# Swapping the quadrants of a matrix by DMA: transfers of consecutive rows, and transfers of every eighth row

## The chip, the cores and the metric

The kernel runs on one core of one Trainium2 chip. It uses none of the core's compute engines for the work itself: the data goes from device memory (HBM) to device memory through the core's 16 DMA engines. The metric is the device time of one execution in microseconds; a kernel's figure is the median of several executions.

## The reference

The input is one float32 matrix of 8192 rows and 8192 columns, 268.44 MB (a row is 32 KB). The reference is

```python
def reference(x: np.ndarray) -> np.ndarray:
    return np.fft.ifftshift(x)
```

With even sizes this shifts both axes by half: the upper left quadrant of 4096 x 4096 changes places with the lower right one, and the upper right with the lower left. Nothing is computed. Half a row, 4096 floats or 16 KB, is the longest run that stays together both in the input and in the output, and every one of the 16,384 half rows moves to another place.

## The kernel before

The program is one loop with no tiles in on-chip memory and no arithmetic. It names four things: `hr` and `hc`, half the number of rows and of columns (4096 each), `col`, the column half of the upper output rows that is being written, and `other`, the opposite column half.

The outer loop (line 28) goes over the upper 4096 output rows in blocks of `ROWS_PER_DMA` = 512 rows, eight blocks. The inner loop (line 29) goes over the two column halves. Each pass issues two transfers. The one on the sync engine's queue (line 31) writes the block in the upper half of the output, from the input rows 4096 further down and the other column half. The one on the scalar engine's queue (line 35) writes the mirror image: the same block of rows in the lower half of the output, from the upper half of the input. So there are 8 x 2 = 16 transfers on each queue, each of 512 half rows of 16 KB, 8 MB in all. Inside a transfer the half rows lie 32 KB apart, on the reading and on the writing side, since the other half of each row belongs to the next transfer of the queue. The second pass of the inner loop takes the same rows with the column halves exchanged.

The order of the work is set by the two queues alone. The two engines issue their transfers in program order, and both queues are served by the same 16 DMA engines. No transfer needs data from another. Each queue has four completion semaphores in turn; a transfer that takes one up again waits until the transfer four places before it on the queue has landed. A transfer ends with one completion write from each of the 16 DMA engines. At the end of the program (the end of the block that begins at line 64) the sync engine waits for the last transfers. Lines 53 and 64 belong to the launch code, which also fills four small constants at the start.

Of the kernel before, what the change touches and what calls it, by code (L numbers as in the profile page):

```python
# [1 line left out]

# [4 lines left out]


ROWS_PER_DMA = 512  # L10


@with_exitstack
def kernel(
    ctx: ExitStack,
    tc: tile.TileContext,
    x: bass.AP,
    out: bass.AP,
):


    nc = tc.nc

    R, C = x.shape
    hr = R // 2
    hc = C // 2

    for row in range(0, hr, ROWS_PER_DMA):
        for col in (0, hc):
            other = hc - col  # L30
            nc.sync.dma_start(
                out=out[row : row + ROWS_PER_DMA, col : col + hc],
                in_=x[row + hr : row + hr + ROWS_PER_DMA, other : other + hc],
            )
            nc.scalar.dma_start(
                out=out[row + hr : row + hr + ROWS_PER_DMA, other : other + hc],
                in_=x[row : row + ROWS_PER_DMA, col : col + hc],
            )


# [1 line left out]
_INS = ['x']  # L42
_OUTS = [((8192, 8192), 'float32')]


def kernel(**inputs):
    import numpy as _np
    import concourse.bacc as _bacc
    import concourse.tile as _tile
    from concourse import mybir as _mybir  # L50
    from concourse.bass_utils import run_bass_kernel_spmd as _run

    nc = _bacc.Bacc("TRN2", target_bir_lowering=False, num_devices=1)  # L53
    arrays, args = {}, []
    for name in _INS:
        a = _np.ascontiguousarray(inputs[name])
        if a.dtype.kind in "iu":
            a = a.astype(_np.int64)
        arrays[f"in_{name}_dram"] = a
        args.append(nc.dram_tensor(f"in_{name}_dram", a.shape, _mybir.dt.from_np(a.dtype), kind="ExternalInput").ap())  # L60
    for i, (shape, dtype) in enumerate(_OUTS):
        dt = _mybir.dt.from_np(_np.dtype(dtype))
        args.append(nc.dram_tensor(f"out_{i}_dram", shape, dt, kind="ExternalOutput").ap())
    with _tile.TileContext(nc) as tc:
        kernel(tc, *args)
    r = _run(nc, [arrays], core_ids=[0])
    got = tuple(r.results[0][f"out_{i}_dram"] for i in range(len(_OUTS)))
    return got[0]
```

## Time and profile before

| what | value |
|---|---|
| median of 4 runs | 812.24 us (811.9 to 812.93) |
| the profiled execution's own time | 812.93 us |
| its span, first to last instruction | 811.1 us |
| DMA packets | 16,896, with 268.44 MB read and as much written |
| mean rate, each byte counted once | 331 GB/s |
| rate of reads and writes together | 662 GB/s |
| transfers | 16 on each of two queues, 8192 KB each |
| median time from issue to landing | 201.5 us (sync), 201.6 us (scalar) |

The profile is of one execution. The span is cut into 40 equal slices of about 20 us; the row marked DMA gives the mean busy share of the 16 engines in tenths (9 means 90% or more), the row marked GB/s what they moved, with each byte counted once. A packet here is one half row of 16 KB, or a completion write of a few bytes. The share of a queue is the time that its packets took as a part of 16 engines' span. The trace also holds, for each packet, its start, duration, size and queue, and for each transfer the times of its 16 completion writes. It holds no addresses. The issue list gives the median time from the issue of a transfer to its landing.

### The profile page before, as it was taken

To read this page: it belongs to the slowest core of one execution; us is meant where nothing else is said; L and a number is where in the kernel's file an instruction comes from. 1 tells how busy PE (TensorE), PEld (TensorE's weight loads), DVE (VectorE), ACT (ScalarE), POOL (GpSimd) and SP (SyncE) were. 2 spreads that over 40 slices of the span, in tenths; PEclk is the share of its full clock that TensorE was granted. 3 is DMA by queue.
4 is the path that set the end of the run, shared out by engine and by line. 5 is a ranking of instruction groups with operands and counts; after the bars stand their busy time and mean duration, and the time that the engine had idled before them with its cause. 6 is when DMAs were issued, how large, how long until landed. Compare 5 with 4: busy or idle time off the path is not lost. (4 is left out here: it accounts for less than half of the span.)

```text
span 811.1 us, 77 instructions
## 1 busy us (share of the span) xinstructions
POOL 0.2 (0%) x4
## 2 busy tenths in 40 slices
POOL 0000000000000000000000000000000000000000
DMA  9999999999999999999999999999999999999998
GB/s 309 333 330 334 335 329 327 339 330 334 335 328 334 334 334 330 334 338 333 334 333 330 336 335 337 332 334 331 331 337 330 332 334 328 330 334 334 337 335 271
DMA packets 16896, 268.44 MB, mean 331 GB/s; under 512 B 512, under 2 KB 512, under 8 KB 512
## 3 DMA queue, kind: packets, MB, share of 16 engines
q1 hardware_dynamic: 8448, 134.22, 50.4%
q10 hardware_dynamic: 8448, 134.22, 48.8%
HBM read 268.44 MB, written 268.44 MB: 662 GB/s over the span
## 5 line engine op out<-in xcount | busy, mean ns | idle before, releaser
L53 POOL MEMSET const-bfloat16-1.0<- 128x1 bf16 x1 | 0.1, 103 | 0.0
L53 POOL MEMSET const-uint8-127<- 128x1 uint8 x1 | 0.1, 103 | 0.0
L53 POOL MEMSET const-float32-1.0<- 128x1 f32 x1 | 0.1, 100 | 0.0
L53 POOL MEMSET const-float32-0.0<- 128x1 f32 x1 | 0.1, 99 | 0.2 <-issue 0.2
## 6 DMA issues: line engine op xcount, KB each, us to landing
out_dram<-in_x_dram ACTq DMA_DIRECT2D x16, 8192.0 KB, 201.6
out_dram<-in_x_dram SPq DMA_DIRECT2D x16, 8192.0 KB, 201.5
```

The lines of the kernel that those rows point to most:

```text
L53: nc = _bacc.Bacc("TRN2", target_bir_lowering=False, num_devices=1)
```

## The change

The number of transfers, their size and the queue of each output half stay as they are. What changes is which rows make up one transfer. Before, a transfer takes 512 consecutive rows of one column half, 32 KB apart. After, it takes every eighth row of the upper (or lower) 4096 rows: 512 rows that lie `STEP * C` = 65,536 floats, 256 KB, apart, so that one transfer reaches over the whole height of its half. The outer loop runs over the eight starting rows `c`, the inner one over the two column halves, and for each the sync queue gets the upper output half and the scalar queue the lower one. The access patterns are written by hand from an offset and the dimensions `dims`: 512 rows with the 256 KB step, and 4096 consecutive floats of each.

```diff
-ROWS_PER_DMA = 512
+STEP = 8
...
-    for row in range(0, hr, ROWS_PER_DMA):
+    dims = [[STEP * C, hr // STEP], [1, hc]]
+    for c in range(STEP):
         for col in (0, hc):
-            other = hc - col
-            nc.sync.dma_start(
-                out=out[row : row + ROWS_PER_DMA, col : col + hc],
-                in_=x[row + hr : row + hr + ROWS_PER_DMA, other : other + hc],
-            )
-            nc.scalar.dma_start(
-                out=out[row + hr : row + hr + ROWS_PER_DMA, other : other + hc],
-                in_=x[row : row + ROWS_PER_DMA, col : col + hc],
-            )
+            for eng, r0, h in ((nc.sync, 0, col), (nc.scalar, hr, hc - col)):
+                eng.dma_start(
+                    out=bass.AP(out.tensor, out.offset + (r0 + c) * C + h, dims),
+                    in_=bass.AP(x.tensor, x.offset + (hr - r0 + c) * C + hc - h, dims),
+                )
```

## The prediction

> **What bounds the kernel now.** I read the page's head and its second and third parts first, to see whether anything but transfers takes time, then the DMA issues, the waits of the sync engine's queue, and the transfer rate in chosen windows.
>
> ```profile
> span 811.1 us, 77 instructions
> ...
> POOL 0.2 (0%) x4
> ...
> DMA  9999999999999999999999999999999999999998
> GB/s 309 333 330 334 335 329 327 339 330 334 335 328 334 334 334 330 334 338 333 334 333 330 336 335 337 332 334 331 331 337 330 332 334 328 330 334 334 337 335 271
> DMA packets 16896, 268.44 MB, mean 331 GB/s; under 512 B 512, under 2 KB 512, under 8 KB 512
> ...
> q1 hardware_dynamic: 8448, 134.22, 50.4%
> q10 hardware_dynamic: 8448, 134.22, 48.8%
> HBM read 268.44 MB, written 268.44 MB: 662 GB/s over the span
> ...
> out_dram<-in_x_dram ACTq DMA_DIRECT2D x16, 8192.0 KB, 201.6
> out_dram<-in_x_dram SPq DMA_DIRECT2D x16, 8192.0 KB, 201.5
> ```
>
> No engine computes; the 16 DMA engines have a packet in flight for 50.4 + 48.8 = 99.2% of the span. The packets are 16,384 rows of 16 KB and 512 small ones (32 transfers, each ending in 16 completion writes). 99.2% of 16 x 811.1 us over 16,384 packets is 786 ns a packet. So the time is the number of packets times the packet's duration, over 16; nothing else is on the path except the ends.
>
> ```profile
> SPq L64 <- DMA out_dram<-in_x_dram: 164.8, 2, 117.5
> SPq L31 <- DMA out_dram<-in_x_dram: 128.9, 12, 49.6
> ```
>
> The sync queue waits, but for transfers four places back: its first four issue without waiting, the other 12 once an earlier one has landed. With 201.5 us from issue to landing and one landing about every 50 us on each queue, the engines never run dry. These waits cost nothing.
>
> Next the windows: stretch, length, the only busy engine, clock, DMA share, GB/s (each byte counted once).
>
> ```profile
> 2.00:4.00 2.00, 0.00 (x0) 1.00 0.99 360
> 4.00:6.00 2.00, 0.00 (x0) 1.00 1.07 385
> 6.00:10.00 4.00, 0.00 (x0) 1.00 0.95 340
> 10.00:20.00 10.00, 0.00 (x0) 1.00 1.00 329
> 20.00:800.00 780.00, 0.00 (x0) 1.00 1.00 333
> 552.00:556.00 4.00, 0.00 (x0) 1.00 0.93 291
> 556.00:560.00 4.00, 0.00 (x0) 1.00 1.11 393
> ```
>
> The middle 780 us run at 333 GB/s; the rest of the span is 31.1 us of ends. The packet records behind these rows say what sets the rate. The shortest 16 KB packet takes 608 ns and 39% take under 650; the median is 727, the 75th percentile 906, the 90th 1,066, the mean 785. A DMA engine that met nobody would take about 611 ns, so about 174 ns of each packet is waiting in memory on other packets. This is the only term that the change can touch.
>
> **The change part by part.** *Count, size, issue.* 8 offsets x 2 column halves x 2 queues are again 32 transfers of 512 rows of 16 KB: the same bytes and packets, 16 issues a queue, the same two queues and alternation of column halves. Cost zero, covered by the four transfers queued ahead. Were the cover gone, an issue plus the start of its packets would show: the first issue begins at 0.73 us, the first packet at 2.20, so 1.5 us a transfer.
>
> *The wait between transfers.* The tail is alike: the last landings, at 808.5 us (sync) and 810.3 (scalar), would again be those of 8 MB transfers whose 16 completions come within 1.1 to 3.5 us of each other. Cost zero.
>
> *The rows in flight together.* This is the change. Those 1.1 to 3.5 us are one or two steps of an engine, which takes a row from each queue every 2 x 786 ns: the 16 engines walk their 32 rows nearly in step. The profile has no addresses, so how rows are dealt is open. If in blocks, engines now stand 32 rows = 1 MiB apart and step by 32 KB; afterwards 8 MiB apart, stepping by 256 KB. If in turn, 32 KB becomes 256 KB between engines. Either way, in one stage of about 100 us (two column halves of one offset) every row read or written on both queues afterwards has the same place, one in eight, within its 256 KB. Now the places in use at one moment differ by the engines' spread and by the sync queue's lead over the scalar queue (about 4 to 5 us in landings, near three steps), and over a transfer all eight come up. If place in 256 KB helps choose which part of memory serves a row, the change makes more rows meet there; the higher address bits must then keep them apart.
>
> No row of this profile has a 256 KB step, so I bound the price. From below: every packet at the unhindered 611 ns gives 16,384 x 0.611 / 16 = 626 us, too far to be a case; every packet at the median, 727, gives 744. From above: at the 75th percentile, 928 us; at the 90th, 1,092. To each belongs the 6.8 us of span without packets (811.1 - 804.3, the packet times summed over 16). The nearer rows are stretches of this same mix. Of the 195 windows of 4 us between 20 and 800 us (291 and 393 above are near the extremes; counting packets by when they end) the slower half averages 323 GB/s, the faster half 343, the fastest quarter 349. I take the slower half as a lasting state: 780 x 333 / 323 = 804.1 us in the middle, plus 31.1 of ends = 835.2 us span, +24.1. It means 24 ns more waiting per packet, 174 to 198: a seventh more contention. I choose the loss over the gain because the edit removes variety among the addresses in flight and adds none that I can name; and the small end of loss because the engines drift freely and can move out of each other's way.
>
> Outside the span the profiled execution has 812.93 - 811.1 = 1.8 us, and it stands 0.7 above the median of the four runs, 812.24. So 835.2 + 1.8 - 0.7 = 836 us.
>
> Two pages of the Trainium skill bear on the size. "DMA: Bandwidth & Descriptors", section "Latency and other measured facts", reports that copies of 16 KiB rows lose rate at large power-of-two pitches (207 GB/s at 512 KiB, 164 at 2 MiB, 103 at 4 and 8 MiB, 214 with a padded pitch), and calls the cause, streams in step on the same memory channels, an inference. Taking its mildest loss, 207/214, an estimate by that page would be 839 us; taking the 8 MiB figure for the distance between engines would double the time. "HBM Reference", section "Specifications (TRN2)", gives about 716 GB/s per memory domain; the 662 read above is 92% of it, and by that figure no order of rows could bring the transfers below some 750 us.
>
> **The rivals.**
> *Faster: the wider step keeps engines apart.* Place: the 174 ns of waiting in the middle stretch. For it: the first full window, when all engines have just started in step, runs at 385 GB/s and the rate falls to 329 by 10 to 20 us, so arrangement matters and the present mix is not the best. Against it: a 2 us window scatters by 25 GB/s, so 385 is two such scatters. Price at the faster half's rate: 780 x 333 / 343 + 31.1 = 788.4, less 22.7, so 790 us; at the fastest quarter's, 776. It decides as soon as the mean packet falls under 784 ns.
> *No change: the addresses are mixed well anyway.* For it: the 20 us slices, all between 324 and 338, show no dependence on where in the matrix the transfers are. 812 us.
> *Deep conflict.* The rows of a stage fall on few parts of memory and the engines cannot drift out of it. For it: 8 MiB between engines leaves only high address bits to tell them apart. Against it: the engines have four transfers queued, so one that falls behind need not hold the others. Price: from the 75th to the 90th percentile packet, 936 to 1,100 us with what lies around.
> *The transfers of a queue wait for each other*, because their row ranges now interlace and the framework sees a conflict. Each of 15 later transfers on a queue would then add the 1.5 us start and up to 3 us of ragged end: 68 us, 880 us in all, or nothing where the other queue fills the gap. Against it: the two column halves of a transfer pair interlace already, and the first four issues a queue do not wait.
>
> **How the numbers follow.** About 0.2%, 1.6 us, is what a measurement here can tell from no change. Moderately slower, 814 to 940: 0.45. Deep conflict, above 940: 0.12. Queue waits: 0.03. No change: 0.10. Faster: 0.30, of which 0.06 lies below 777, the fastest quarter's rate. Slower is then 0.60, same 0.10, faster 0.30. The range 777 to 940 leaves out 0.18. Of the slower cases alone the likeliest's own range is 814 to 940, the upper end the 75th percentile packet.
>
> **What would show it.** Right: 16,896 packets and x16 issues of 8192 KB a queue as now, the DMA row still all 9s, the shortest packet still near 608 ns, but the slices around 323 GB/s instead of 333 and fewer packets under 650 ns. Wrong in sign: slices above 335 with more packets at the floor. Zeros or dips in the DMA row at each landing, or waits on the transfer just before, would mean queue waits. A rate that changes with the offset stage, about every 100 us, would show that the place in 256 KB matters by itself. The forecast fails most easily at the sign: it rests on an argument about addresses that no row here shows.

## The result and the profile after

The changed kernel takes 811.38 us (median of 53 executions, 810.79 to 812.47), the kernel before 813.61 us in the same comparison (79 executions, 809.0 to 819.31). The ratio is 0.9972, 95% interval 0.9964 to 0.998: faster by 0.28% (2.2 us between the medians), just beyond what such a measurement can tell from no change. The forecast was 836 us, slower. Ratios given with an interval compare the faster executions of each kernel, so they can differ from the ratio of the medians.

The difference is one of steadiness: of the 79 executions of the kernel before, 56 are slower than the slowest of the changed kernel (812.47 us), but 7 are faster than its fastest (810.79 us).

These are the rows of the page of the changed kernel that answer to those shown of before: head, busy share of the DMA engines, rate, packets, queues and issues.

```profile
span 809.8 us, 77 instructions
...
DMA  9999999999999999999999999999999999999999
GB/s 308 330 333 334 332 333 333 328 334 335 335 333 333 331 337 329 336 331 337 319 337 333 337 334 333 333 333 335 329 334 334 333 330 337 335 333 331 337 329 302
DMA packets 16896, 268.44 MB, mean 332 GB/s; under 512 B 512, under 2 KB 512, under 8 KB 512
...
q1 hardware_dynamic: 8448, 134.22, 49.8%
q10 hardware_dynamic: 8448, 134.22, 49.8%
HBM read 268.44 MB, written 268.44 MB: 663 GB/s over the span
...
out_dram<-in_x_dram ACTq DMA_DIRECT2D x16, 8192.0 KB, 201.5
out_dram<-in_x_dram SPq DMA_DIRECT2D x16, 8192.0 KB, 201.4
```

Packets, issues and the time to landing are as they were. The difference is in the last slice (302 GB/s against 271 before) and in the queue shares: the packets' time, 99.6% of 809.8 = 806.6 us, is 2.0 us more than before (99.2% of 811.1 = 804.6), and the part of the span without packets (averaged over the 16 engines) falls from 6.5 to 3.2 us. The net is the 1.3 us between the spans.

The windows of the changed kernel (stretch, length, busy engine, clock, DMA share, GB/s) say the same.

```profile
2.00:4.00 2.00, 0.00 (x0) 1.00 0.99 287
4.00:6.00 2.00, 0.00 (x0) 1.00 1.06 434
6.00:10.00 4.00, 0.00 (x0) 1.00 1.02 356
10.00:20.00 10.00, 0.00 (x0) 1.00 1.00 326
20.00:800.00 780.00, 0.00 (x0) 1.00 1.00 333
800.00:812.00 12.00, 0.00 (x0) 1.00 0.64 217
```

The last row has this counterpart before:

```profile
800.00:812.00 12.00, 0.00 (x0) 1.00 0.61 206
```

The middle moves at 333 GB/s in both. Between the 1,000th and the 16,000th half row to end, the packet records give 333.14 GB/s before and 333.06 after. The completion times of the last transfer on each queue show what became of the end (us from the span's start; first, median and last of the 16 engines):

```
              sync queue              scalar queue
before   805.0   805.7   808.5    807.3   808.1   810.3
after    806.0   806.5   806.8    807.9   808.6   808.9
```

The typical engine of the changed kernel finishes a little later, its last engine 1.4 us earlier. This holds all the way through: the 16 completions of a transfer lie 1.1 to 3.5 us apart before and 0.5 to 1.4 us after. The sync queue's waits did not change in kind.

```profile
SPq L62 <- DMA out_dram<-in_x_dram: 165.1, 2, 117.2
SPq L33 <- DMA out_dram<-in_x_dram: 131.6, 12, 50.0
```

So for this pair of executions the gain is at the end. It is not the whole story, as three more traces of the kernel before show below.

### The profile page after: what moved, and what is told of

Same layout as the page of the kernel before. It is cut to its first block, busy times and chain, and to the rows that moved or that the text cites. A ratio compares the mean times of both kernels' runs of the same rounds, so it can differ in the third digit from the quotient of the medians.

```text
span 809.8 us, 77 instructions
## 1 busy us (share of the span) xinstructions
POOL 0.2 (0%) x4
```

## The experiments

Each comparison is with the kernel before on the same chip; its median beside the first group (the next four runs) was 822.17 us, beside the others 813.5 to 814.7. The record gives the same chip number, 8, for the first group and for one of the later ones, so why the first is 1% slower (329 GB/s in the middle of its two traces of the same row order, in place of 333) is open; that shift is larger than the gain of the change, and the changed kernel itself was not run there. The diffs are shortened: a loop and its body stand on one line, and `move(start, dims)` stands for the changed kernel's two inner loops, with the starting row and the access pattern as arguments. In a pattern such as `[[256 * C, 16], [C, 32], [1, hc]]` the first pair makes 16 groups of rows, 256 rows apart, the second the 32 rows of a group; the rows of a group are taken to go to one engine (in the run with eight groups eight engines took part). The step between the rows that an engine takes one after another is called its walk.

```diff
+    def move(start, dims):
         for col in (0, hc):
             for eng, r0, h in ((nc.sync, 0, col), (nc.scalar, hr, hc - col)):
                 eng.dma_start(
-                    out=bass.AP(out.tensor, out.offset + (r0 + c) * C + h, dims),
-                    in_=bass.AP(x.tensor, x.offset + (hr - r0 + c) * C + hc - h, dims),
+                    out=bass.AP(out.tensor, out.offset + (r0 + start) * C + h, dims),
+                    in_=bass.AP(x.tensor, x.offset + (hr - r0 + start) * C + hc - h, dims),
                 )
```

**Groups 8 MiB apart, walking 32 KB.**

```diff
-    for c in range(8): move(c, [[8 * C, 512], [1, hc]])
+    for b in range(8): move(32 * b, [[256 * C, 16], [C, 32], [1, hc]])
```

> Each transfer takes 16 groups of 32 consecutive half rows, the groups 8 MiB apart: the spacing between engines of the changed kernel if rows are dealt in blocks, with the 32 KB step of the kernel before. Theory A (shared ceiling: memory gives all reads and writes together about 666 GB/s, whichever rows are in flight): the middle stays at 333 GB/s and the time within 0.4% of before, 809 to 815 us; only the ends can differ. Theory B (which rows meet sets the rate, and the 256 KB step happens to be as good as 32 KB): a new mix gives a new rate, more than 1% away. If the wide spacing between engines is what lets them finish together, the 16 completion writes of a transfer come within about 1 us of each other, as in the changed kernel (0.5 to 1.4 us), and the time is about 0.2 to 0.3% below before; if the 256 KB step is the cause, they spread to about 3 us as before and the time is that of before.

Measured: 1,802.33 us (median of six executions, 1,753 to 1,882), 2.19 times before by the medians; the ratio of the faster executions is 2.136 (2.1266 to 2.1454). The completions of a transfer lie 3.1 to 5.1 us apart. The page of an execution of 1,808 us:

```profile
span 1806.6 us, 77 instructions
...
DMA  8989999999999999999989899999999999999999
GB/s 143 159 147 150 147 147 153 141 151 146 145 153 142 152 150 147 155 146 158 142 149 153 139 157 145 152 150 147 151 144 150 152 144 155 150 145 151 148 153 135
DMA packets 16896, 268.44 MB, mean 149 GB/s; under 512 B 512, under 2 KB 512, under 8 KB 512
...
HBM read 268.44 MB, written 268.44 MB: 297 GB/s over the span
```

The engines are as busy as ever with as many packets, but a 16 KB packet takes 1,742 ns on average instead of the 785 of before. The same bytes through the same queues, in another order of addresses, take twice the time: the plain ceiling (theory A) falls as the whole account, and the deep conflict that the prediction kept as a rival exists. It also makes it unlikely that the changed kernel has its engines 8 MiB apart; a later run tests this.

**A block's rows dealt in turn, 32 KB between engines.**

```diff
+    for b in range(8): move(512 * b, [[C, 16], [16 * C, 32], [1, hc]])
```

> The blocks of 512 consecutive rows of the kernel before, but row r of a block goes to group r mod 16: 16 groups 32 KB apart, each stepping by 512 KB, so that engines in step work within 512 KB of memory. Theory A (shared ceiling): 333 GB/s in the middle, 809 to 815 us. Theory B (which rows meet sets the rate): this is the arrangement furthest from both kernels, and the rate moves by more than 1% in one direction. On the ends: if an engine lags because its rows always have the same place among 16 MiB (rows dealt in blocks of 1 MiB), the completions come closer together than the 3 us of before, since each engine now meets all places within 16 MiB at a 512 KB step; if not, they stay near 3 us.

Measured: 822.79 us, ratio 1.0004 (0.9983 to 1.0024); completions 1.0 to 3.1 us apart. The rate is that of before. Nothing in it separates it from the kernel before.

**14 engines.**

```diff
+    for b in range(8): move(504 * b, [[42 * C, 12], [C, 42], [1, hc]])
+    move(4032, [[4 * C, 16], [C, 4], [1, hc]])
```

> Transfers of 504 consecutive rows, split in 12 groups of 42 so that only 12 DMA engines take part (64 rows at the end go to all 16). Theory A (shared ceiling): 12 engines at the unhindered 611 ns a half row could move 322 GB/s, just under the ceiling of 333, so the packets shorten: mean packet between 611 and 680 ns, 834 to 930 us in all, far less than a third more. Theory C (786 ns is an engine's own pace): packets stay at 786 ns and the time is 16/12 of before, about 1,075 us.

Measured: 874.46 us, ratio 1.0641 (1.0605 to 1.0676). The run is not what its expectation describes. The 12 groups of 42 adjacent rows merge into one list of 504 rows: the trace describes each of these transfers with a single dimension of 504. The 512 small packets (32 transfers of 14 and 4 of 16) show that 14 engines took part.

```profile
span 866.3 us, 81 instructions
...
DMA  7888888888888888888878888788788878875554
GB/s 292 325 324 327 326 329 330 333 323 331 325 326 332 328 328 325 328 326 324 331 296 331 327 329 322 295 324 308 301 322 326 323 282 318 328 289 240 216 216 191
DMA packets 16896, 268.44 MB, mean 310 GB/s; under 512 B 512, under 2 KB 512, under 8 KB 512
```

For the first half, after the first slice, 14 engines move 323 to 333 GB/s, as 16 do beside it (329 in the middle of the next run). Over the whole run a packet takes 692 ns on average, and 72% of them are under 650. The time is lost later: the 14 completions of one transfer lie 9 us apart at first and up to 115 us later, so some engines run far ahead and are out of work at the end. Theory C, 786 ns as an engine's own pace, would have given 822.17 x 16 / 14 = 940 us.

**Eight groups, undone by merging.**

```diff
+    for b in range(8): move(512 * b, [[64 * C, 8], [C, 64], [1, hc]])
```

> The blocks of the kernel before, split in 8 groups of 64 rows, so that 8 DMA engines take part. Theory A (shared ceiling): 8 engines at 611 ns move 214.5 GB/s, well under 333, so nearly every packet takes 611 ns: about 1,251 us plus 5 of ends, 1,256 us. Theory B (rows that meet): fewer rows meet, some waiting stays; mean packet between 611 and 700 ns, 1,256 to 1,440 us. Theory C (an engine's own pace): 786 ns a packet, about 1,610 us.

Measured: 822.08 us, that of before. The 8 groups of 64 adjacent rows also merge into a list of 512 (a single dimension in the trace), and 16 engines work as before. The run says nothing on its question.

**The changed kernel's rows, blocks written out.** With 31 rows of 32 in a group the pattern cannot merge.

```diff
+    for c in range(8): move(c, [[256 * C, 16], [8 * C, 31], [1, hc]])
+    move(248, [[256 * C, 16], [C, 8], [1, hc]])
```

> The changed kernel's rows with the dealing written out: 16 groups 8 MiB apart, each of 31 rows at a 256 KB step, so that the pattern can't be merged into one list of 512 rows; the 32nd rows go in four transfers of 128 rows at the end. Theory D (a list of 512 rows isn't dealt in blocks of 32, so the changed kernel never had its engines 8 MiB apart): this kernel is slow like the run with groups 8 MiB apart and a 32 KB step, about 2.1 times before. Theory E (the changed kernel is dealt in blocks, and the 256 KB step is what keeps the engines apart): about the time of the changed kernel, within 1% of before.

Measured: 1,496.94 us (1,463 to 1,609 in four executions), 1.84 times the 813.49 of before by the medians.

```profile
HBM read 268.44 MB, written 268.44 MB: 361 GB/s over the span
```

Theory D stands: dealt in blocks of 32, the changed kernel would be slow. Against the first run, with a step of 32 KB inside a block, it loses less (1.84 against 2.19 by the medians), but the wider step does not rescue it.

**The changed kernel's rows dealt in turn.**

```diff
+    for c in range(8): move(c, [[8 * C, 16], [128 * C, 32], [1, hc]])
```

> The changed kernel's transfers, but row r of a transfer goes to group r mod 16: groups 256 KB apart, stepping by 4 MiB. Theory D with rows dealt in turn: the same as the changed kernel, 0.2 to 0.3% below before, its completions within 0.5 to 1.4 us. Theory E (blocks): another arrangement, so its completions or its rate differ from the changed kernel's; if the shared ceiling holds for it, the middle still has the rate of before.

Measured: 811.59 us, ratio 0.997 (0.9942 to 0.9998), completions 0.6 to 1.2 us apart: the changed kernel again, in time and in trace. With the run before it, a list of 512 rows behaves as rows dealt in turn: row r goes to engine r mod 16. The kernel before is likewise matched by its rows dealt in turn (1.0004, above). So the engines stand 32 KB apart in the kernel before and 256 KB apart in the changed one. The trace has no addresses, so this is by likeness of kernels, not seen directly.

**Blocks of 1 MiB written out.**

```diff
+    for b in range(8): move(512 * b, [[32 * C, 16], [C, 31], [1, hc]])
+    move(31, [[32 * C, 128], [1, hc]])
```

> The kernel before with blocks written out: 16 groups 1 MiB apart of 31 consecutive rows; the 32nd rows go in four transfers of 128 rows at the end. If a list of 512 rows is dealt in blocks (Theory E): the time of before within 0.5%, completions spread by about 3 us. If it is dealt in turn (Theory D) this is a new arrangement, and tells whether 1 MiB between engines meets the conflict of 8 MiB: 1.0 times before if only larger distances do, clearly slower if 1 MiB does too.

Measured: 980.55 us (972 to 1,036), ratio 1.2012 (1.1944 to 1.2081).

```profile
HBM read 268.44 MB, written 268.44 MB: 519 GB/s over the span
```

So the kernel before isn't dealt in blocks either, and 1 MiB between engines already meets the conflict.

**8 MiB less one row.**

```diff
-    for b in range(8): move(32 * b, [[256 * C, 16], [C, 32], [1, hc]])
+    for b in range(7): move(32 * b, [[255 * C, 16], [C, 32], [1, hc]])
+    move(224, [[255 * C, 16], [C, 31], [1, hc]])
+    move(4080, [[C, 16], [1, hc]])
```

> The slow run's groups of 32 consecutive rows at a 32 KB step, but 255 rows apart instead of 256, that is 8 MiB less 32 KB; the last 16 rows go in transfers of their own. If the exact power of two puts the engines' rows on the same part of memory (Theory F): the shift by one row takes them apart, and the rate is back at about that of before, within 3%. If the distance itself is the cost, whatever its low bits: still about 2.1 times before.

Measured: 842.18 us, ratio 1.0365 (1.0314 to 1.0415), against 2.136 with 256 rows.

```profile
GB/s 295 316 323 321 321 318 323 321 316 324 324 324 314 325 320 323 326 323 319 321 319 321 321 324 322 323 322 326 314 321 319 317 320 323 321 320 320 323 321 282
```

One row less between the engines takes nearly all of the conflict away: at 8 MiB it belongs to the power of two, not to the distance. The rest, 321 GB/s in place of 333, misses the 3% that was expected and is not explained. Other distances were not tried with a row less.

**Eight engines.**

```diff
+    for b in range(8): move(512 * b, [[C, 8], [8 * C, 64], [1, hc]])
```

> The blocks of 512 consecutive rows of the kernel before, dealt in turn to 8 groups (row r to group r mod 8, 64 rows each), so that only 8 DMA engines take part. Theory A (memory has a ceiling near 666 GB/s of reads and writes together, and the 174 ns of waiting in a packet is that ceiling shared out): 8 engines at 611 ns move 214.5 GB/s, far below it, so the median packet is 611 ns, the mean at most 640, and the time 1,256 to 1,315 us. Theory C (786 ns is an engine's own pace for these rows): about 1,610 us.

Measured: 1,249.63 us, one execution.

```profile
span 1247.8 us, 77 instructions
...
DMA packets 16640, 268.44 MB, mean 215 GB/s; under 512 B 256, under 2 KB 256, under 8 KB 256
...
q1 hardware_dynamic: 8320, 134.22, 25.1%
q10 hardware_dynamic: 8320, 134.22, 25.1%
HBM read 268.44 MB, written 268.44 MB: 430 GB/s over the span
```

The 256 small packets are 32 transfers of 8, so half the engines worked. Now 99.9% of the 16 KB packets take under 650 ns, and the mean is 611. The 174 ns of waiting is gone with half the load: it is not an engine's own pace but what 16 engines take from each other at 666 GB/s of reads and writes. Theory C falls, and the ceiling stands for engines whose rows keep clear of the conflict. Whether the limit is the memory's own or that of the way to it, no run separates.

**128 KB between engines.**

```diff
+    for b in range(0, 4096, 2048):
+        for c in range(4): move(b + c, [[4 * C, 16], [64 * C, 32], [1, hc]])
```

> Rows dealt in turn with 128 KB between engines, stepping by 2 MiB; 512 rows a transfer and 16 transfers a queue as in both kernels. Known so far: 32 KB between engines (before) 1.000, 256 KB 0.997. Theory A (ceiling for all distances that keep the engines apart): within 0.5% of before. On the ends: if the completions close up with growing distance, their spread lies between the 3 us of 32 KB and the 1 us of 256 KB, and the time between the two kernels'.

Measured: 810.59 us (810.0 to 811.75), ratio 0.9962 (0.9939 to 0.9985); completions 0.8 to 1.5 us apart, 333.5 GB/s in the middle. The rate and the spread came as expected; the time, expected between the two kernels', can't be told from the changed one's.

**512 KB between engines.**

```diff
+    for c in range(16): move(c, [[16 * C, 16], [256 * C, 16], [1, hc]])
```

> Rows dealt in turn with 512 KB between engines, stepping by 8 MiB; 256 rows a transfer, 32 transfers a queue. This is the next distance above the changed kernel's 256 KB and below the 1 MiB that, in the run with written-out blocks, cost 20%. If the conflict sets in gradually with distance: 2 to 15% slower than before. If it sets in between 512 KB and 1 MiB, or belongs to the 32 KB walk of the blocks and not to the distance: within 0.5% of before.

Measured: 858.52 us, ratio 1.0544 (1.0507 to 1.0581).

```profile
DMA  9999999999999999999999999999999999999998
GB/s 292 312 315 316 311 316 315 316 313 319 312 318 316 316 315 311 313 314 319 315 319 317 314 317 313 316 314 318 313 316 313 317 318 310 317 318 313 318 313 282
...
HBM read 268.44 MB, written 268.44 MB: 628 GB/s over the span
```

The whole middle is down to 315 GB/s. With the 20% at 1 MiB, the conflict sets in gradually, one doubling above the changed kernel. Two other things changed with the distance: transfers are half as large (4 MB, 32 a queue), and an engine's own walk has steps of 8 MiB, where 4 MiB cost nothing. The DMA share stays full, which speaks against idle time between transfers; the walk of 8 MiB is not separated from the distance.

**One queue.**

```diff
-            for eng, r0, h in ((nc.sync, 0, col), (nc.scalar, hr, hc - col)):
-                eng.dma_start(
+            for r0, h in ((0, col), (hr, hc - col)):
+                nc.sync.dma_start(
```

> The changed kernel's 32 transfers, all on the sync engine's queue, alternately for the upper and the lower output half. Theory A (memory's ceiling): four transfers ahead on one queue keep the engines full, so the middle stays at 333 GB/s and the time within 0.4% of the changed kernel. If the two queues alternating on an engine cost or save something of the 174 ns, the rate moves by more than 1%.

Measured: 811.32 us, ratio 0.9968 (0.9943 to 0.9993). Beside the changed kernel's 811.38 us, the split of the output halves over two queues is worth nothing that can be told.

**The kernel before, three more traces.** No edit.

> The kernel before, once more, for its trace. If the gain of the change is at the ends alone: 333 GB/s between packets 1,000 and 16,000, whatever the time, completions of the last transfers 2.5 to 3.5 us apart, and executions differ by 3 us at most. If the middle of the kernel before varies by itself: an execution of 815 us or more has 331 GB/s or less in the middle, one of 810 us 333.5 or more.

> The kernel before, a second trace beside the one just named, with the same expectations: ends alone, or a middle rate that follows the time.

> The kernel before, a third trace, with the same expectations: ends alone, or a middle rate that follows the time.

Measured: 811.73, 816.57 and 812.0 us. The middle window of the first and of the second:

```profile
20.00:770.00 750.00, 0.00 (x0) 1.00 1.00 333
```

```profile
20.00:770.00 750.00, 0.00 (x0) 1.00 1.00 331
```

From the 1,000th to the 16,000th half row the three give 333.48, 331.13 and 333.19 GB/s, and the completions of the last transfer on the scalar queue lie 2.9, 1.6 and 2.7 us apart. So the kernel before does both: in two of three it has the full rate and a ragged end, in the third a rate 0.7% lower from 20 us to the end, worth some 5 us, and a more even end. Ends alone are ruled out as the whole account. Of the 79 executions of the kernel before in the result, 47 took over 813 us, longer than any execution that was traced at the full rate (811.73 to 812.93), so the lower rate is probably common; that is inferred, for one trace alone shows it.

**64 KB between engines.**

```diff
+    for b in range(0, 4096, 1024):
+        for c in range(2): move(b + c, [[2 * C, 16], [32 * C, 32], [1, hc]])
```

> Rows dealt in turn with 64 KB between engines, stepping by 1 MiB; 512 rows a transfer, 16 transfers a queue. Distances known so far: 32 KB 1.000 with executions 11 us apart and completions about 3 us apart at the end, 128 KB 0.9962 and 256 KB 0.997 with executions under 2 us apart and completions about 1 us apart. If steadiness comes with distance gradually: between them, executions 3 to 8 us apart, 0.997 to 1.0. If 32 KB is the odd one, because there the engines' rows share a stretch of 512 KB of consecutive rows: as at 128 KB, 0.996 to 0.997, executions under 2 us apart.

Measured: 810.73 us (809.99 to 811.88), ratio 0.997 (0.9952 to 0.9989), completions 1.3 to 2.4 us apart. The executions are as steady as at 128 KB, so 32 KB is the odd one; the completions close up gradually. That the rows at 32 KB share one stretch of 512 KB, the reason that the expectation gives, is not tested.

Together, by distance between the rows that the 16 engines work on at one time (the 1.84 is of the medians, the other ratios are those given above):

| distance | how dealt | time against before |
|---|---|---|
| 32 KB (before) | list of 512, in turn | 1 |
| 32 KB | in turn | 1.0004 |
| 64 KB | in turn | 0.997 |
| 128 KB | in turn | 0.9962 |
| 256 KB (after) | list of 512, in turn | 0.9972 |
| 512 KB | in turn, 8 MiB walk, 4 MB transfers | 1.0544 |
| 1 MiB | blocks, 32 KB walk | 1.2012 |
| 8 MiB | blocks, 256 KB walk | 1.84 |
| 8 MiB | blocks, 32 KB walk | 2.136 |
| 8 MiB less 32 KB | blocks, 32 KB walk | 1.0365 |

No kernel here beats the changed one by more than can be told: 128 KB has the shortest median, 810.59 us, 0.1% below 811.38.

## Why the prediction was wrong

*What bounds the kernel*: right, and now shown. Packets times duration over 16 is the time, an unhindered packet takes 611 ns (eight engines), and the other 174 ns is what the engines take from each other. That this waiting is "the only term that the change can touch" was wrong: the ends moved too.

*Count, size, issue; the waits between transfers*: right. Packets, issues, waits and time to landing did not move.

*The tail, "Cost zero"*: wrong, and it holds the gain of the profiled pair. The step took for granted that the completions would again come within 1.1 to 3.5 us of each other. They come within 0.5 to 1.4, and the last lands at 808.9 in place of 810.3.

*The rows in flight together*: this step failed, at "the edit removes variety among the addresses in flight". It left open how rows are dealt and then priced a loss, 780 us at 323 GB/s, of a kind that shows only from 512 KB between engines on. The loss of 24.1 us did not come: the middle ran its 780 us at 333 GB/s again. The runs say dealt in turn: the engines went from 32 KB to 256 KB apart, and between these distances the middle has the ceiling, 333 GB/s. That all rows of a stage have the same place in 256 KB costs nothing here: the mean packet went from 785 to 788 ns, not to 809. Nor was the price that of a lasting state: 323 and 343 GB/s are the halves of a scatter of 4 us windows around one rate, which over 20 us shrinks to 324 to 338.

*The sign*: the packets did change, but evenly. Under 650 ns went from 39% to 30%, the 90th percentile from 1,066 to 1,005 ns: fewer free, fewer badly delayed, nearly the same mean. That fits a ceiling that is shared more fairly and engines that finish together; that fairness is the cause of the even end is argued, not shown.

*The rivals*: "no change" came nearest, 812 us against 811.38, and for the middle its account holds too: no slice shows a dependence on the place in the matrix. "Faster" had the right sign by the wrong mechanism: it needed a mean packet under 784 ns, and the mean rose. Its evidence, the opening window of 385 GB/s, was the start itself: from 2 to 10 us the rows average 356 GB/s before and 358 after, and both kernels have 333 later. "Deep conflict" is real, from 512 KB between engines on (5%), and the change stopped one doubling short of it. The queue waits did not come.

*The pages of the Trainium skill*: "DMA: Bandwidth & Descriptors", section "Latency and other measured facts", has copies slowing with power-of-two row pitch, and a pad of a few KiB restoring them. The runs agree in kind: 5% at 512 KB, 2.1 times at 8 MiB, nearly all of it back with one row less. In a list dealt in turn the pitch of the rows is the distance between the engines, and that is the distance which counted here. A pitch of 4 MiB along one engine's own walk, which the changed kernel has when dealt in turn, cost nothing. "HBM Reference", section "Specifications (TRN2)", gives about 716 GB/s; the best middle here, 2 x 333.5 = 667, is 93% of it.

What stays open: what makes distances of 512 KB and more slow, beyond that it goes with the power of two at 8 MiB; and why the kernel before has the full rate in some executions and 0.7% less in others, while 64, 128 and 256 KB between engines have it in every trace (one of 64, one of 128, three of 256). The place of the two matrices in memory was not varied. How the 2.2 us between the medians divide between that and the ends is not settled: the ends gave 1.4 us in one pair.

## What to carry to other kernels

Before pricing a new stride, ask which addresses the 16 engines hold at the same moment: a list of rows behaved as dealt in turn, so the stride of the list is the distance between engines. Power-of-two distances of 512 KB and more between them cost 5% to a factor of two here, and at 8 MiB one row off the power of two gave most of it back. Where packets wait on each other at a ceiling, here 666 GB/s of reads and writes, no order of rows and no use of queues that was tried raised it: what the better orders gained was steadiness and an even end.

## What the runs showed that was not expected

Pattern dimensions that are adjacent in memory merge before rows are dealt: 12 groups of 42 rows became one list on 14 engines, 8 groups of 64 one list on 16. Fourteen engines reach the rate of sixteen, 323 to 333 GB/s in the first half, but share it unevenly, so that a transfer's completions come to lie up to 115 us apart and the time is 6.4% longer; why they do is open. And the distance of 32 KB, the plainest order of rows, is the least steady of those at the ceiling: executions of the kernel before spread over 10 us, those at 64, 128 and 256 KB over less than 2 us each.
